# An attention stage written as 32 steps with a fixed order on each engine

## The chip, the cores and the metric

The kernel runs on one core of a Trainium2 chip. The metric is the time of one execution in device microseconds, the median of several runs. TensorE (PE in the profile) multiplies and transposes, and writes only to PSUM, here eight banks of 128 x 512 float32; VectorE (DVE) and ScalarE (ACT) read PSUM and work beside it; GpSimd (POOL) works on SBUF alone. SyncE (SP) issues most DMAs, GpSimd some. Each engine runs its own list of instructions one after the other and waits at semaphores for the others. The names DVE, ACT, POOL, PE, PEld (TensorE's weight loads) and SPq are those of the profile.

## What is computed

One layer of an encoder over 1024 rows of 1024 float32: half a SwiGLU, a mixer, half a SwiGLU, a norm. The change lies in the second part of the mixer.

```python
x = x + 0.5 * swiglu_half_step(x, ffn1_norm, ffn1_w_in, ffn1_w_out)
x = x + hybrid_mixer(x, ...)          # concatenate([attn, rec]) @ w_out
x = x + 0.5 * swiglu_half_step(x, ffn2_norm, ffn2_w_in, ffn2_w_out)
x = rms_norm(x, final_norm)

s = einsum('bqkgd,bskd->bkgqs', q_blk, k)      # 4 query heads, 2 key heads of 128
o = einsum('bkgqs,bskd->bqkgd', softmax(s), v)
attn = rms_norm(o, attn_out_gain)              # over the 512 columns of all heads
rec = rms_norm(recurrence) * silu(g)           # four heads of 128 columns
```

## The kernel before, in words

Every float32 product is made of three matmuls on rounded halves (high x high, high x low, low x high), so nearly every evacuation of PSUM is a pair: ScalarE copies or scales the high half (`hi`), VectorE subtracts it from the source for the low half (`lo`).

The program is written in order and planned by the framework's scheduler at build time: it lists instructions by priority (the order of the text, with stretches under `high_priority` ahead) and fills engines as its own time estimate has them free. What the engines execute is that order. `behind(x)` (line 96) adds an edge: an instruction is issued after `x` on the same engine. A tile pool hands out its buffers by tag; a tile waits until the buffer's former tile is done with.

The stage around the change:

- `mixer_in` (line 1043) ends the input projections. Its last one, `rg_av`, makes four parts (`rgv_ps`, line 831) in PSUM tag `pp` (four banks) and empties each with a Silu of the recurrence's gate (`gate`, line 1081) and a split of v into `v_attn` (line 1120). The gate goes through one of two buffers of `st` and is stored by SyncE (line 1086).
- `attention` (line 1132) opens its pools over that memory: SBUF starts with two buffers `rg` on the two of `st`, then `x1` (one), `rT`, three `p`, `qT`, `qr`; in PSUM two banks of tag `b` and two of tag `o` on the old `pp`, and two double banks `pp` for the scores.
- 32 pairs `seq[i] = (tp, n, tt)`: four blocks `tp` of 256 query rows, four heads `n`, two halves `tt` of 128 rows. For each: six score matmuls into a `pp` tile, the maximum (VectorE, line 1187), the exponential (ScalarE, 1190), the reciprocal and the scaling of p by GpSimd (left half) and ScalarE (right half); two groups of four transposes of p through tag `b` (`transposed`, 1197, with copy and subtraction into pT); after two `tt` the product with v (`values`, 1208: 24 matmuls of 256 columns), whose sum of squares over the heads makes the norm (`attn_scale`, 1284). The scores of pair i + 2 stand ahead of the transposes of pair i.
- The output projection of the recurrence (`rec_out`, 1265) goes with pairs 0 to 7: load the rows of the four recurrence heads and of the gate into `rg`, multiply on GpSimd, transpose (`rT`, tag `o`), project with `w_out`'s lower half (`project`, 1233: two halves of twelve matmuls, tag `o`), add to the row block x1 and store as x2.
- The output projection of attention (`attn_out`, 1292) of block `tp` goes with the pairs of the next block: load x2, project with the upper half (`woa`, loaded and split at pairs 4, 6, 9 and 10), scale and add on VectorE, store x3 from GpSimd's queue; `to_ffn` (1308) norms the row block for the second FFN and stores xn2. The last two row blocks follow the loop.
- The queries of the next block are transposed as a whole in a `pp` tile (`q_tile`, 1158).
- Then the second FFN opens its own pools over all of this, loads xn2 and weights, and transposes the rows (`pt_ffn_B`).

## Time and profile before

| | |
|---|---|
| median of three runs | 1928.17 us (1928.05 to 1928.54) |
| the profiled execution | 1929.75 us; its span, first to last instruction, 1927.6 |
| granted clock of TensorE, mean | 0.999 |
| TensorE, weight loads, VectorE, ScalarE, GpSimd busy | 99%, 83%, 65%, 42%, 37% of the span |
| the attention stage | from about 1052 to 1276.6 us of the span |

How it is read: times count from the first instruction. A row of a timeline gives start, length, engine, line, operation, written and read tile, shape and count; in brackets stands how long the engine was idle before it and who ended that. A row of the waits gives the total, the number and the longest of one kind. A row of the chain is a piece of the path that ended last, in order of time. [...]

### The profile page before, as it was taken

How to read it: one execution, taken by the hardware profiler on the slowest of the kernel's cores; microseconds unless marked ns; L12 is line 12 of the kernel's file. 1: busy time of each engine (PE TensorE's matmuls, PEld its weight loads, DVE VectorE, ACT ScalarE, POOL GpSimd, SP SyncE). 2: the span in 40 equal slices, each digit the busy share in tenths (PEclk: the TensorE clock that was granted, in tenths of full speed). 3: DMA queues.
4: the chain of work that ended last, by engine and by line, in shares of the span. 5: the costliest groups of instructions: out<-in, count | busy, mean ns of one | idle time of the engine just before them, and what ended most of it. 6: DMA issues, size and time to landing. Idle time of an engine off the chain costs nothing.

```text
span 1927.6 us, 26292 instructions
## 1 busy us (share of the span) xinstructions
PE 1905.8 (99%) x10025; PEld 1597.7 (83%) x10025; DVE 1250.9 (65%) x1578; ACT 802.1 (42%) x1280; POOL 714.1 (37%) x561
## 2 busy tenths in 40 slices
PE   9999999999999999999999999999999999999998
...
DMA packets 212940, 254.78 MB, mean 132 GB/s; under 512 B 13495, under 2 KB 140748, under 8 KB 212814
## 3 DMA queue, kind: packets, MB, share of 16 engines
...
q8 instruction: 79, 1.29, 0.3%
...
## 4 chain that ended last, share of the span: by engine, by line
PE 90%; DVE 4%; DMA 3%; issue 1%; ACT 1%; POOL 0%; SPq 0%; DVEq 0%; POOLq 0%; ACTq 0%
PE pa_ffn L298 17%; PE pd_ffn L298 11%; PE pya_ffn L684 7%; PE rec_ps L166 6%; PE pc_ffn L298 6%; PE pb_ffn L298 6%; PE pp_ffn L280 5%; PE pye_ffn L684 3%; PE pyd_ffn L684 3%; PE pyc_ffn L684 3%; PE aq_ps L831 2%; PE ri_ps L831 2%; PE pa L1243 2%; PE rgv_ps L831 2%; PE pv L1215 2%; PE s L1183 2%
## 5 line engine op out<-in xcount | busy, mean ns | idle before, releaser
L94 DVE TENSOR_TENSOR hl_in_ffn_A<-raw_in_ffn,hl_in_ffn_A 128x512 fp32r<-128x512 f32 x120 | 177.4, 1478 | 94.0 <-ACT hl_in_ffn_A L93 93.9
L298 PE MATMUL pa_ffn<-ffn_T,hl_in_ffn_S 128*128 128x512 f32 x960 | 236.8, 389 | 0.0
L298 PE MATMUL pd_ffn<-ffn_B,hl_in_ffn_S 128*128 128x512 f32 x936 | 225.7, 389 | 0.0
L298 PEld LDWEIGHTS pa_ffn<-ffn_T,hl_in_ffn_S 128*128 128x128 f32 x960 | 180.2, 188 | 37.4
L298 PEld LDWEIGHTS pd_ffn<-ffn_B,hl_in_ffn_S 128*128 128x128 f32 x936 | 175.7, 188 | 36.4
L93 ACT CAST hl_in_ffn_S<-s_ffn 128x512 fp32r<-128x512 f32 x160 | 99.0, 622 | 212.2 <-PE pd_ffn L298 159.0
L94 DVE TENSOR_TENSOR hl_in_ffn_S<-s_ffn,hl_in_ffn_S 128x512 fp32r<-128x512 f32 x160 | 140.9, 885 | 70.7 <-ACT hl_in_ffn_S L93 70.5
L94 DVE TENSOR_TENSOR hl_out_ffn_A<-raw_out_ffn_A,hl_out_ffn_A 128x1024 fp32r<-128x1024 f32 (+1 forms) x66 | 101.6, 1551 | 48.1 <-ACT hl_out_ffn_A L93 47.3
L93 ACT CAST hl_in_ffn_A<-raw_in_ffn 128x512 fp32r<-128x512 f32 x120 | 74.9, 625 | 137.1 <-PE pc_ffn L298 70.8
L94 DVE TENSOR_TENSOR hl_out_ffn_S<-raw_out_ffn_S,hl_out_ffn_S 128x512 fp32r<-128x512 f32 (+1 forms) x88 | 101.6, 1162 | 40.7 <-ACT hl_out_ffn_S L93 40.7
L166 PE MATMUL rec_ps<-hm,hl_rec_w 128*128 128x512 f32 x528 | 123.1, 392 | 0.8 <-DVE hm L145 0.4
L254 POOL TENSOR_TENSOR s_ffn<-s_ffn,raw_in_ffn 128x512 f32<-128x512 f32 x40 | 63.5, 1587 | 159.5 <-issue 104.6
L684 PE MATMUL pya_ffn<-hl_out_ffn_S 128*128 128x512 f32 x528 | 120.9, 390 | 0.1
L298 PE MATMUL pa_ffn<-ffn_B,hl_in_ffn_A 128*128 128x512 f32 x480 | 116.9, 389 | 0.0
L684 PEld LDWEIGHTS pya_ffn<-hl_out_ffn_S 128*128 128x128 f32 x528 | 99.0, 188 | 21.4 <-DVE hl_out_ffn_S L94 1.0
L166 PEld LDWEIGHTS rec_ps<-hm,hl_rec_w 128*128 128x128 f32 x528 | 98.4, 188 | 21.7 <-DVE hm L145 0.8
L298 PE MATMUL pc_ffn<-ffn_T,hl_in_ffn_A 128*128 128x512 f32 x480 | 115.9, 389 | 0.0
L298 PE MATMUL pb_ffn<-ffn_B,hl_in_ffn_A 128*128 128x512 f32 x480 | 115.3, 389 | 0.0
L93 ACT CAST hl_out_ffn_S<-raw_out_ffn_S 128x512 fp32r<-128x512 f32 (+1 forms) x88 | 73.4, 837 | 95.7 <-PE pya_ffn L684 38.6
L298 PEld LDWEIGHTS pc_ffn<-ffn_T,hl_in_ffn_A 128*128 128x128 f32 x480 | 90.1, 188 | 18.7
L298 PEld LDWEIGHTS pb_ffn<-ffn_B,hl_in_ffn_A 128*128 128x128 f32 x480 | 90.1, 188 | 18.7
L298 PEld LDWEIGHTS pa_ffn<-ffn_B,hl_in_ffn_A 128*128 128x128 f32 x480 | 90.0, 188 | 18.7
...
## 6 DMA issues: line engine op xcount, KB each, us to landing
...
raw_out_ffn_S<-d_comb SPq DMA_DIRECT2D x88, 256.0 KB, 2.7
d_comb<-g_ffn POOLq DMA_DIRECT2D x80, 256.0 KB, 2.3
raw_out_ffn_A<-d_act SPq DMA_DIRECT2D x66, 256.0 KB, 5.1
ffn_kept<-in_ffn_w_out SPq DMA_DIRECT2D x65, 256.0 KB, 5.4
d_act<-g_ffn SPq DMA_DIRECT2D x60, 256.0 KB, 2.3
raw_out_ffn_A<-in_ffn_w_out SPq DMA_DIRECT2D x52, 256.0 KB, 5.4
...
```

The lines of the kernel that those rows point to most:

```text
L93: nc.scalar.copy(hl[:, 0, :], src)
L94: (lo_engine or nc.vector).tensor_sub(hl[:, 1, :], src, hl[:, 0, :].bitcast(F32))
L166: nc.tensor.matmul(out, hl[:, a, ks], h[half][b][:, k, cols], start=(k == 0 and i == 0), stop=(k == NK - 1 and i == 2),)
L254: nc.gpsimd.tensor_sub(s2, s1, a11)
L280: nc.tensor.matmul(halves(ps[j]), A[2 * j + k // 4][:, a, ks], B[k // 4][:, :, b, k % 4, lo:hi], start=(k == 0 and i == 0), stop=(k == NK ...
L298: nc.tensor.matmul(ps, A[:, a, ks], op(key)[:, b, k, :], start=(first and k == 0 and i == 0), stop=(k == 3 and i == 2), skip_group_check=True,
L684: nc.tensor.matmul(ps, hl[:, a, j * P : (j + 1) * P], hl[:, b, hi], start=(first and i == 0 and n == 0), stop=(i == last and n == 2), skip ...
L831: nc.tensor.matmul(ps[:, tt, :], h[half][a][:, k, ts], hl[j][:, b, ws], start=(k == 0 and i == 0), stop=(k == NK - 1 and i == 2),)
L1183: nc.tensor.matmul(ps[:, ks], qT[:, a, qs], kT[:, b, kv, ks], start=(i == 0), stop=(i == 2))
L1215: nc.tensor.matmul(ps, vt[:, j, a, vs], pT[j][:, b, i4, :], start=(st == 0 and i == 0), stop=(st == NT - 1 and i == 2),)
L1243: nc.tensor.matmul(py, lhs(a, n), units[n][:, b, ds], start=(n == 0 and i == 0), stop=(n == 3 and i == 2),)
```

## The change

The 32 pairs become 32 steps, and each compute instruction of the loop is issued through `run`, which puts it behind the last one of its engine: the order of the text is the order on TensorE, VectorE, ScalarE and GpSimd. The prologue is issued through `free`, without that edge. DMAs are still placed by the scheduler. Each step gives the order: scores of step i + 2 (first half), first transposes, scores (second half), the product with v of the pair before (even steps, one step later than before), output halves, the transposes for the recurrence's next block and for the next block's queries, second transposes. Tables at the top say in which step what goes: the recurrence's blocks, the loads and the splits of `woa`, and each half of attention's output projection.

Besides: the queries are transposed in two halves through tag `b`, in the steps with i % 8 of 2 and 4; `values` uses tag `o` always; `x1` has two buffers; `woa` is loaded without the gate on a load, two or three steps ahead of its split; residual rows (x2) are asked for a step ahead of their use, those of the last two blocks in step 30 and behind the loop; the store of the gate's last two parts of the second column group goes by GpSimd's queue; the last two row blocks take three heads first and the fourth once the last product with v is there.

```diff
+REC_STEPS = (0, 1, 3, 4, 5, 7, 9, 11)
+WOA_LOADS = (2, 5, 8, 10)
+WOA_LATE = {4: 0, 7: 1, 11: 2, 12: 3}
+ATTN_HALVES = (13, 15, 16, 17, 19, 21, 23, 25, 27, 27, 29, 29)
...
-            nc.sync.dma_start(
+            (nc.gpsimd if (c, part // 2) == (1, 1) else nc.sync).dma_start(
...
+        last = {}
+        def run(engine, fn, *args, **kw):
+            with self.behind(last.get(engine)):
+                last[engine] = fn(*args, **kw)
+            return last[engine]
+        def free(engine, fn, *args, **kw):
+            return fn(*args, **kw)
+        def lows(do, lo, src, hi):
+            do("dve", nc.vector.tensor_sub, lo, src, hi.bitcast(F32))
+        def request(r0, j, name):
+            raw = self.wpool.tile([P, 1024], F32, name=f"raw_{name}{j}", tag="raw")
+            nc.sync.dma_start(raw, w_out[r0 + j * P : r0 + (j + 1) * P, :])
+            return raw
+        def cast(raw, j, pool, tag):
+            hl = pool.tile([P, 2, 1024], F32R, name=f"hl_woa{j}", tag=tag)
+            run("act", nc.scalar.copy, hl[:, 0, :], raw)
+            lows(run, hl[:, 1, :], raw, hl[:, 0, :])
+            return hl
...
-            pt = self.ps(f"qTp{tp}")
...
+        def q_turn(do, tp, raw, half, tag):
+            pt = self.ps(f"qTp{tp}_{half}", tag)[:, :512]
+            for m in range(2):
                 for tt in range(2):
+                    i = tt * 512 + (2 * half + m) * P
+                    at = slice(m * 256 + tt * P, m * 256 + (tt + 1) * P)
+                    do("pe", nc.tensor.transpose, pt[:, at], raw[:, i : i + P], self.ident)
+            hi, lo = (qT[tp][:, j, half * 512 : (half + 1) * 512] for j in range(2))
+            def evacuate():
+                do("act", nc.scalar.copy, hi, pt)
+                lows(do, lo, pt, hi)
+            return evacuate
...
+        def scores(do, a, j):
+            if j == 0:
+                a.ps = self.ps(f"s{a.nm}")
+            ks = slice(j * 512, (j + 1) * 512)
+            for i, (x, y) in enumerate(((0, 0), (0, 1), (1, 0))):
+                do("pe", nc.tensor.matmul, a.ps[:, ks], qT[a.tp][:, x, a.qs], kT[:, y, a.kv, ks],
+                   start=(i == 0), stop=(i == 2))
+        def small(a, what):
+            return self.stat.tile([P, 1], F32, name=f"{what}{a.nm}", tag=what)
+        def exponential(do, a):
+            neg_max, a.den = small(a, "nmax"), small(a, "den")
+            do("dve", nc.vector.tensor_reduce, neg_max, a.ps, AX.X, ALU.max, negate=True)
+            a.p = s4(f"p{a.nm}", "p")
+            do("act", nc.scalar.activation, a.p, a.ps, AF.Exp, bias=neg_max, accum_out=a.den)
+        def inverse(do, a):
+            a.rd = small(a, "rd")
+            do("dve", nc.vector.reciprocal, a.rd, a.den)
+            do("pool", nc.gpsimd.tensor_scalar_mul, a.p[:, 0:512], a.p[:, 0:512], a.rd)
+        def scaled(do, a):
+            do("act", nc.scalar.mul, a.p[:, 512:], a.p[:, 512:], a.rd)
+        def turned(a, j):
+            pt = self.ps(f"ptp{a.nm}_{j}", "b")
             for t in range(4):
                 i = (j * 4 + t) * P
+                run("pe", nc.tensor.transpose, pt[:, t * P : (t + 1) * P], a.p[:, i : i + P], self.ident)
             src = pt.rearrange("p (s t) -> p s t", t=P)
+            hi, lo = (a.pT[:, j, i, :, a.tt * P : (a.tt + 1) * P] for i in range(2))
+            def evacuate():
+                run("act", nc.scalar.copy, hi, src)
+                lows(run, lo, src, hi)
+            return evacuate
+        def values(a):
...
+            def evacuate():
+                run("act", nc.scalar.mul, hi, ps, g)
+                run("dve", nc.vector.scalar_tensor_tensor, out=lo, in0=ps, scalar=g, in1=hi.bitcast(F32),
+                    op0=ALU.mult, op1=ALU.subtract)
+                if a.n == 0:
+                    run("act", nc.scalar.activation, sq, ps, AF.Square)
+                    return
+                s1 = pools["sq"].tile([P, 256], F32, name=f"sq{a.nm}", tag="sq")
+                run("act", nc.scalar.activation, s1, ps, AF.Square)
+                engine = ("dve", nc.vector) if a.tp == 3 else ("pool", nc.gpsimd)
+                run(engine[0], engine[1].tensor_add, sq, sq, s1)
+            return evacuate
+        def half_out(py, lhs, units, ds, heads=range(4)):
+            for n in heads:
+                for i, (x, y) in enumerate(((0, 0), (0, 1), (1, 0))):
+                    run("pe", nc.tensor.matmul, py, lhs(x, n), units[n][:, y, ds],
+                        start=(n == 0 and i == 0), stop=(n == 3 and i == 2))
...
+        def rec_turn(t):
+            rg = rows[t][0]
+            run("pool", nc.gpsimd.tensor_mul, rg[:, 0:512], rg[:, 0:512], rg[:, 512:])
             pt = self.ps(f"rT{t}", "o")
             for n in range(NREC):
                 ns = slice(n * P, (n + 1) * P)
+                run("pe", nc.tensor.transpose, pt[:, ns], rg[:, ns], self.ident)
+            rT = recT[t] = pools["rT"].tile([P, 2, 512], F32R, name=f"recT{t}", tag="rT")
+            def evacuate():
+                run("act", nc.scalar.mul, rT[:, 0, :], pt, self.rec_gain)
+                run("dve", nc.vector.scalar_tensor_tensor, out=rT[:, 1, :], in0=pt, scalar=self.rec_gain,
+                    in1=rT[:, 0, :].bitcast(F32), op0=ALU.mult, op1=ALU.subtract)
+            return evacuate
+        def rec_half(t, dd):
+            py = self.ps(f"py{t}_{dd}", "o")
+            half_out(py, lambda x, n: recT[t][:, x, n * P : (n + 1) * P], rec_units, cols(dd))
+            x1 = rows[t][1][:, cols(dd)]
+            def evacuate():
+                run("dve", nc.vector.tensor_add, x1, py, x1)
+                if dd:
+                    nc.sync.dma_start(d["x2"][t], rows[t][1])
+            return evacuate
+        def out_scale(tp, do=run, tag="o"):
             pss = self.ps(f"oss{tp}", tag)
             for tt in range(2):
+                do("pe", nc.tensor.matmul, pss[:, tt : tt + 1], ssq[tp][:, tt * P : (tt + 1) * P], self.ones,
+                   start=True, stop=True)
+            work = self.stat.tile([P, 2, 2], F32, name=f"rs_ao{tp}", tag="rs2")
+            scale[tp] = work[:, 1, :]
+            def evacuate():
+                do("dve", nc.vector.tensor_scalar, work[:, 0, :], pss[:, 0:2], 1.0 / (NQ * HD), EPS,
+                   ALU.mult, ALU.add)
+                do("pool", nc.gpsimd.tensor_tensor, out=work[:, 1, :], in0=work[:, 0, :],
+                   in1=self.neg_half[:, :2], op=ALU.pow)
+            return evacuate
+        def row(t):
+            rows[NT + t] = x = s4(f"x2_{t}", "xs")
             nc.sync.dma_start(x, d["x2"][t])
...
+        def attn_half(t, dd):
+            py = self.ps(f"pa{t}_{dd}", "o")
+            half_out(py, lhs_attn(t), units, cols(dd))
+            def evacuate():
+                attn_add(t, dd, py)
+                if dd:
+                    nc.gpsimd.dma_start(d["x3"][t], rows[NT + t])
+            return evacuate
+        def to_ffn(t):
+            x = rows[NT + t]
             xn = pools["xn"].tile([P, D], F32, name=f"xn_n2_{t}", tag="xn")
+            ss = self.stat.tile([P, 1], F32, name=f"ss_n2_{t}", tag="ss1")
+            run("act", nc.scalar.activation, xn, x, AF.Square, accum_out=ss)
+            work = self.stat.tile([P, 2, 1], F32, name=f"rs_n2_{t}", tag="rs1")
+            run("dve", nc.vector.tensor_scalar, work[:, 0, :], ss, 1.0 / D, EPS, ALU.mult, ALU.add)
+            run("pool", nc.gpsimd.tensor_tensor, out=work[:, 1, :], in0=work[:, 0, :],
+                in1=self.neg_half[:, :1], op=ALU.pow)
+            def finish():
+                run("dve", nc.vector.scalar_tensor_tensor, out=xn, in0=x, scalar=work[:, 1, :], in1=gain2,
+                    op0=ALU.mult, op1=ALU.mult)
+                nc.gpsimd.dma_start(d["xn2"][t], xn)
+            return finish
...
+        waiting, finishing, raw_q, raw_w = None, [], None, {}
         for i, (tp, n, tt) in enumerate(seq):
+            a, u = steps[i], i % 8
+            ahead = step(i + 2) if i + 2 < len(seq) else None
             if tt == 0:
+                pT = self.hpool.tile([P, 2, 2, 4, 256], F32R, name=f"pT{a.nm}", tag="h")
+            a.pT = pT
+            if u == 0 and tp < 3:
+                raw_q = q_load(tp + 1)
+            if i in WOA_LOADS:
+                j = WOA_LOADS.index(i)
+                raw_w[j] = request(0, j, "woa")
+            if i == 0:
+                rec_turn(0)()
+            if tp and u == 2:
+                out_scale(tp - 1)()
+            if ahead:
+                scores(run, ahead, 0)
+            turned(a, 0)()
+            if ahead:
+                scores(run, ahead, 1)
+            if i and i + 1 < len(seq):
+                scaled(run, steps[i + 1])
+            if ahead:
+                exponential(run, ahead)
+            after = []
+            if tt == 0 and waiting:
+                after.append(values(waiting))
+                waiting = None
+            outs = []
+            if i in REC_STEPS:
+                t = REC_STEPS.index(i)
+                if t + 1 < NT:
+                    rows[t + 1] = rec_loads(t + 1)
+                outs = [rec_half(t, dd) for dd in range(2)]
+            elif i in ATTN_HALVES:
+                outs = [attn_half(*divmod(m, 2)) for m, at in enumerate(ATTN_HALVES) if at == i]
+            later = []
+            if i + 1 in REC_STEPS:
+                later.append(rec_turn(REC_STEPS.index(i + 1)))
+            if tp < 3 and u in (2, 4):
+                later.append(q_turn(run, tp + 1, raw_q, u // 2 - 1, "b"))
+            tb = turned(a, 1)
+            for f in outs:
+                f()
+            if ahead:
+                inverse(run, ahead)
+            for f in (*after, *((tb, *later) if tt else (*later, tb)), *finishing):
+                f()
+            finishing = []
+            if i + 1 in ATTN_HALVES[::2]:
+                row(ATTN_HALVES[::2].index(i + 1))
+            if i - 1 in ATTN_HALVES[1::2]:
+                finishing.append(to_ffn(ATTN_HALVES[1::2].index(i - 1)))
+            if i == len(seq) - 2:
+                row(2 * tp)
+            if i in WOA_LATE:
+                j = WOA_LATE[i]
+                units.append(cast(raw_w.pop(j), j, *(gate if j == 3 else whl)))
+            if tt:
+                waiting = a
+        t0 = 2 * (len(seq) // 8 - 1)
+        wide = {}
+        row(t0 + 1)
+        for t in (t0, t0 + 1):
+            wide[t] = self.ps(f"pa{t}")
+            for dd in range(2):
+                half_out(wide[t][:, cols(dd)], lhs_attn(t), units, cols(dd), range(3))
+            if t == t0:
+                values(waiting)()
+        for dd in range(2):
+            half_out(wide[t0][:, cols(dd)], lhs_attn(t0), units, cols(dd), (3,))
+        out_scale(t0 // 2, run, "b")()
+        for dd in range(2):
+            attn_add(t0, dd, wide[t0][:, cols(dd)])
+        nc.gpsimd.dma_start(d["x3"][t0], rows[NT + t0])
+        for dd in range(2):
+            half_out(wide[t0 + 1][:, cols(dd)], lhs_attn(t0 + 1), units, cols(dd), (3,))
+        for dd in range(2):
+            attn_add(t0 + 1, dd, wide[t0 + 1][:, cols(dd)])
+        nc.gpsimd.dma_start(d["x3"][t0 + 1], rows[NT + t0 + 1])
...
-                c3, tc, "m2", rg=2, x1=1, rT=1, p=3, qT=2, qr=1
+                c3, tc, "m2", rg=2, x1=2, rT=1, p=3, qT=2, qr=1
```

## The prediction, made before the changed kernel ran

> **What bounds the kernel now.** The page comes first: its span and its line of TensorE.

> ```profile
> span 1927.6 us, 26292 instructions
> PE 1905.8 (99%) x10025; PEld 1597.7 (83%) x10025; DVE 1250.9 (65%) x1578; ACT 802.1 (42%) x1280; POOL 714.1 (37%) x561
> ```

> The profiled execution took 1929.75 us, 1.58 above the median of the three runs (1928.17); a difference worked out on the trace is added to that median at the end. TensorE is the bound from end to end: an edit can only win what TensorE idles, and costs whatever makes it idle anew. About 0.2% (3.9 us) is what a measurement of this kernel can tell from no change. The change leaves the count of matmuls and transposes alone and orders the attention stage anew, so next comes the stage by itself: busy time by windows, then who TensorE waited for in it.

> ```profile
> 1052.00:1276.60 224.60, 218.01 (x1293) 188.59 (x1292) 137.39 (x212) 123.18 (x221) 77.98 (x70) 1.00 0.41 136
> ```

> ```profile
> PE ptp L1202 <- DVE pT L1206: 3.2, 5, 1.0
> PE s L1183 <- ACT p L1190: 1.0, 2, 0.7
> PE rT L1271 <- issue: 0.9, 1, 0.9
> PE pv L1215 <- DVE pT L1206: 0.7, 2, 0.3
> PE pa L1243 <- ACT oT L1221: 0.6, 1, 0.6
> ```

> The columns behind the length (224.60) are the busy times of TensorE, its weight loads, VectorE, ScalarE and GpSimd. TensorE idles 224.60 - 218.01 = 6.6 us here, and half of it is one wait: the transposes of the probabilities (ptp) wait for VectorE to empty one of the two banks of tag `b`. The true loss is somewhat more. A matmul's record overhangs the start of the next one, so each wait shows short by the overhang. The chain in order of time gives the real pitch:

> ```profile
> 1119.09 2.78 DMA d_x<-x
> 1121.93 5.46 DMA x<-d_x
> ...
> 1161.70 2.88 PE pv L1215 x24
> 1164.58 2.75 PE pa L1243 x12
> ...
> 1173.51 0.87 PE ptp L1202 x8
> ```

> So TensorE spends 2.88 on a `values`, 2.75 on half an output projection (twelve matmuls; so 0.69 on three score matmuls of the same 512 columns), 0.44 on four transposes. Eight transposes are recorded as 1.04 (below) and pitch at 0.87: 0.17 of overhang. Eleven waits in the five rows times 0.17 are 1.9; 6.6 + 1.9 = **8.5 us** is what a perfect order could win, 0.44% of the run. Its ends are 6.6 and about 10 (waits too short for the view).

> **Part 1, what goes.** The two DMA rows above show the store of x2 and then the load of the next x1 standing in the chain, because `x1` has one buffer; the change gives it two and asks for the `woa` rows up to three steps before their split. That, and most of the five rows, is curable by an order. I credit the whole 8.5 and then charge the waits of the new order one by one.

> **Part 2, the entry.** TensorE's new queue begins with the transposes rT(0) into a bank of tag `o`, and everything else of the loop stands behind them. Tag `o` lies on the banks of the last rgv part (pool order: b, o over the old `pp`), which is emptied late:

> ```profile
> 1054.29 2.89 PE L1183 MATMUL s<-kT,qT 128*128 128x512 f32 x12
> 1055.11 0.36 SPq L1086 DMA_DIRECT2D d_g<-rg  x1
> 1055.59 0.69 DVE L94 TENSOR_TENSOR v_attn<-rgv_ps,v_attn 128x512 fp32r<-128x512 f32 x1 [0.91 <-ACT v_attn L93]
> 1058.00 1.80 SPq L1258 DMA_DIRECT2D rg<-d_rec  x4
> 1059.84 0.43 SPq L1260 DMA_DIRECT2D rg<-d_g  x1
> 1064.78 1.29 POOL L1267 TENSOR_TENSOR rg<-rg 128x512 f32<-128x512 f32 x1 [1.32 <-DMA rg<-d_g]
> ```

> Before, twelve score matmuls filled the time from 1054.29. Now they are queued behind rT(0), which waits until 1055.59 + 0.69 = 1056.28, plus 0.13 of release (below): **2.1 us** of idle, with the prologue's other work already done inside rgv.

> The gate stores are costed next. SyncE no longer waits for the last two Silus, so the rows of rg(0) and the second half of k are asked for some us sooner; they are covered by the rgv matmuls, and that is worth nothing to TensorE. But rg(1) lies on the buffer of the last gate part: its load (1058.00) follows that store (1055.11) by 2.9. GpSimd's stores of the same size land like SyncE's:

> ```profile
> d_comb<-g_ffn POOLq DMA_DIRECT2D x80, 256.0 KB, 2.3
> d_act<-g_ffn SPq DMA_DIRECT2D x60, 256.0 KB, 2.3
> ```

> So rg(1) comes when it came. Its last piece takes 3.7 as a median and took up to 1064.78 - 1059.84 = 4.9 here:

> ```profile
> rg<-d_g SPq DMA_DIRECT2D x8, 256.0 KB, 3.7
> ```

> GpSimd multiplies it from 1063.5 to 1064.8 on, 1.29 later rT(1) can start: 1064.8 to 1066.1. TensorE is there at 1056.4 + 0.44 + 2 x 0.69 + 0.44 + 2 x 2.75 = 1064.2, and turned(0,1) is queued behind. Cost 0.7 to 2.0, I take **1.4**. [...]

> **Part 3, the queries in halves.** This is the largest term. The transposes of the next queries moved from `pp` to tag `b`: six times (steps 2, 4, 10, 12, 18, 20) three tiles pass through two banks between `values` and the next step's first transposes. Durations:

> ```profile
> 1240.59 1.13 ACT L1190 ACTIVATE p<-s,nmax 128x1024 f32<-128x1024 f32 x1
> 1241.50 1.22 DVE L1187 TENSOR_REDUCE nmax<-s 128x1 f32<-128x1024 f32 x1
> 1247.45 0.47 ACT L1221 ACTIVATE oT<-pv,cols 128x256 fp32r<-128x256 f32 x1 [1.27 <-PE pv L1215]
> 1249.86 0.40 ACT L1230 ACTIVATE sq<-pv 128x256 f32<-128x256 f32 x1
> 1251.91 1.04 PE L1202 MATMUL ptp<-ident,p 128*128 128x128 f32 x8
> 1252.54 1.07 ACT L1205 CAST pT<-ptp 128x512 fp32r<-128x512 f32 x2 [1.60 <-PE ptp L1202]
> 1253.16 1.29 DVE L1206 TENSOR_TENSOR pT<-ptp,pT 128x512 fp32r<-128x512 f32 x2 [1.67 <-ACT pT L1205]
> 1258.57 1.28 DVE L125 SCALAR_TENSOR_TENSOR xn_n<-x,rs_n,g_ffn_norm 128x1024 f32<-128x1024 f32 x1 [0.70 <-POOL rs_n L86]
> 1260.17 1.28 DVE L1206 TENSOR_TENSOR pT<-ptp,pT 128x512 fp32r<-128x512 f32 x2
> 1260.99 1.16 PE L1202 MATMUL ptp<-ident,p 128*128 128x128 f32 x8 [0.18 <-DVE pT L1206]
> ```

> The fourth transpose of 1251.91 is issued by 1252.35 and ScalarE starts at 1252.54: 0.19. VectorE's subtraction starts 0.62 after the copy and takes 0.69, two of them 1.29 (pitch 0.60). TensorE starts 1260.99 after a subtraction that ended at 1260.86: 0.13. Clock an even step from 0. TensorE: scores 0.69, first transposes 1.13, scores 1.82, `values` 4.70, queries 5.14, second transposes 5.58, next scores 6.27; then the next transposes want the bank of the queries. ScalarE, in its fixed order: copy 1.32; VectorE's subtraction 1.94, maximum 2.54 to 3.76; exponential 3.8 to 4.9; oT 4.93; square 5.3; only then the queries' copy at 5.66, subtraction 6.28 to 6.97, release 7.1. TensorE idles 7.1 - 6.27 = 0.83. That is the floor, 6 x 0.83 = 5.0. In steps 2 and 10 the recurrence's rT (the same 512 columns, one more on each engine) stands in front: about 1.2 each. In step 4 two halves give the engines time, but rT stays in front: 1.0. In step 12 the split of woa2 left over from step 11 (1024 columns, about 1.1 and 1.2 as in the rows of that width above) delays the exponential: 1.9. In 18 and 20 the xn row of 1.28 stands on VectorE ahead of the step's first subtraction: 1.5 each. Sum 8.3 with these lags, 5.0 without; I take **6.5**, the middle, since each lag may be eaten by the stall before it. All other steps hold: two tiles through two banks, a bank wanted five us after it was written.

> [...]

> **Part 4, the last steps.** In step 31 nothing is left to put between: second transposes of step 30, first of 31, second of 31. With `values` ending at V, ScalarE does oT, square and the copy from V + 0.92 on, subtraction V + 1.54 to V + 2.2, release V + 2.35; TensorE is there at V + 0.87. Cost **1.4** (0.8 if ScalarE is ahead). After it nothing waits: the three first heads of row 6, the last `values`, the three first heads of row 7 cover each other's evacuations by 4.1 us of matmuls (eighteen at the pitch above).

> **Part 5, the start of the second FFN.** Row 7's load stands on SyncE until the xn row of 5 is done, and FFN 2's first loads stand behind it, as before:

> ```profile
> 1248.41 11.83 SPq L1296 DMA_DIRECT2D x<-d_x  x2
> 1260.34 0.85 SPq L1545 DMA_DIRECT2D xn<-d_xn  x2
> ...
> 1264.34 3.81 SPq L1545 DMA_DIRECT2D xn<-d_xn  x1
> ...
> 1276.18 1.91 PE L442 MATMUL pt_ffn_B<-ident,xn 128*128 128x128 f32 x16
> ```

> Before, they start at 1260.34, 15.8 ahead of the first transposes of FFN 2. Now that xn row is finished in step 31. From the end of row 5's last half: step 30's copy ends at 5.2, the square of row 5 at 6.4, two more copies 7.6, their subtraction 8.4, xn 9.7. TensorE from there to the end of the stage: five groups of transposes and a `values` 5.1, the 1.4, then 36 + 12 matmuls, a `values` and the sums 14.3, together 20.8; so the loads start some 11 ahead. Against that the wait of 3.81 goes: `x1` has one more buffer, so xn row 2 lands on `rT`'s old place and no longer on a `p` still in use. The first four loads come 4.8 later, the rest about 1. What of that TensorE feels no row shows; between nothing and half the shift, 0 to 2.5, I take **0.6**, nearer to nothing since the weights wait longest for their use.

> Sum: 2.1 + 1.4 + 6.5 + 1.4 + 0.6 = 12.0 of new waits against 8.5 of old ones: **+3.5 us**, 1933.2 for a profiled execution, **1931.7** against the median. The bounds together: 2.1 + 0.7 + 5.0 + 0.8 + 0 - 10 = -1.4 to 2.1 + 2.0 + 8.3 + 1.4 + 2.5 - 6.6 = +9.7.

> **Rivals.** *The order pays.* The queries' bank comes free in time, because ScalarE reaches their copy sooner than I clock it, and rT(1) too; only the entry and 0.7 stay: 2.1 + 0.7 - 8.5 = -5.7, 1922.5. For it: ScalarE is 55% busy in the stage (123.18 of 224.60), and the waits that go are real. Against it: even an idle ScalarE needs 0.19 + 0.62 + 0.69 + 0.13 = 1.63 where TensorE has 1.13 of other work. Chance 0.2.

> *FFN 2's loads decide.* The place is SyncE's queue behind row 7. If the first weights land more than a microsecond behind the end of attention, TensorE waits for each microsecond beyond; the price is the shift of 4.8 on top of the forecast: +8.3, 1936.5. For it: the queue stood 11.83 us in the same place. Against it: the 3.81 that goes. Chance 0.2.

> **How the numbers follow.** The forecast (0.6) is +3.5 with bounds of -1.4 and +9.7; as +3.9 is the limit, I give 0.34 of it to no change and 0.26 to slower. With the rivals: faster 0.20, same 0.34, slower 0.20 + 0.26 = 0.46. The likeliest time is 1931.7. The range goes from 1922.5, which leaves out half of the first rival, to 1937.5, which leaves out under 0.1 above. No change and slower hold most of the chance; the forecast's own range is 1926.8 to 1937.9.

> **What would show it.** Right: the timeline after shows TensorE idle for some 2 us ahead of the first rT, one wait of 0.8 to 1.9 at the first transposes of steps 3, 5, 11, 13, 19 and 21, each ended by a subtraction of qT, and one of 1.4 in step 31; the store and load of x1 are out of the chain; the stage's idle time is 10 us or more. Wrong: the row of ptp waiting for qT is short or absent (then the first rival), or a DMA ends a wait over a microsecond anywhere after step 1 (then the order meets the queues, and the sum is too low).

## The result, and the profile after

The changed kernel is **slower by 1.1%**: 1949.05 us median (1946.35 to 1952.09) against 1928.21 (1928.05 to 1928.54), ratio 1.0108, 95% interval 1.0091 to 1.0126. The forecast was 1931.7 with a range of 1922.5 to 1937.5. The profiled execution took 1952.09, the longest of its four, so the trace below shows some 3 us more than the median. (The four took 1952.09, 1949.41, 1948.68 and 1946.35, at a mean granted clock of 0.993, 0.995, 0.996 and 0.997.) Of all executions below one alone falls out, 6245.39 us in the version with some attention halves moved, without a trace; the ratio there leaves it out.

The page of the changed kernel, its span and busy line:

```profile
span 1950.3 us, 26280 instructions
PE 1912.5 (98%) x10025; PEld 1601.9 (82%) x10025; DVE 1247.8 (64%) x1582; ACT 803.1 (41%) x1284; POOL 721.7 (37%) x563
```

The work of TensorE is the same, the span 22.7 us longer. The attention stage by windows, columns as before (length; busy time of TensorE, its weight loads, VectorE, ScalarE, GpSimd; granted clock):

```profile
1052.00:1298.00 246.00, 225.42 (x1299) 192.97 (x1297) 138.01 (x215) 125.71 (x227) 81.18 (x71) 0.97 0.35 120
```

The stage idles 246.00 - 225.42 = 20.6 us instead of 6.6, and TensorE is busy for 225.4 instead of 218.0 on the same work, at a granted clock of 0.97 instead of 1.00. Both are losses. Whom it waited for (all instructions issued through `run` bear its line, L1145; one goes by tiles):

```profile
PE ptp L1145 <- DVE qT L1145: 6.9, 4, 3.2
PE ptp L1145 <- POOL ssq L1145: 4.2, 2, 2.2
PE rT L1145 <- POOL rg L1145: 3.2, 1, 3.2
PE pt_ffn_B L446 <- DVE x L1145: 2.9, 2, 2.3
PE ptp L1145 <- DVE pT L1145: 1.3, 1, 1.3
PE rT L1145 <- issue: 0.8, 1, 0.8
PE py L1145 <- DVE x L1145: 0.8, 1, 0.8
```

The first two rows are the queries' bank, six times, as forecast, in the steps forecast (in two of them a GpSimd addition ended within 0.1 us of the subtraction of qT and got the name; with the queries in another bank, below, these two waits go as well, though the addition stays). The row of 3.2, five times, by which the kernel before waited for pT is down to one wait, that of step 31, and the store and load of x1 are out of the chain.

To add the losses up I take, for each instruction on TensorE, the distance from the start of the one before it, less the median of that distance for its kind (a wait measured so is called "by starts" below); the sum from the start of the stage to the second FFN's first transposes is 10.9 us before and 28.7 after, in the next 60 us 1.5 and 5.9. That is 22.2 of the 22.7. After, it is mainly: the entry 3.35, the queries' six waits 12.1 (1.67, 0.81, 1.74, 2.40, 3.35, 2.13), three waits for a bank of tag `o` or for recT 2.6, step 31 1.9, the start of the second FFN 3.6 in three waits; and matmuls that run at half pace behind some of these waits, 7.4 in the stage and about 2 in the second FFN. The half pace is in the windows. Three of four and six microseconds, right behind the waits of 1.74, 2.40 and 3.35 (the third column from the end is the granted clock):

```profile
1150.10:1154.10 4.00, 4.00 (x20) 3.39 (x21) 2.35 (x3) 2.06 (x3) 0.00 (x0) 1.00 0.00 0
1166.00:1170.00 4.00, 4.00 (x14) 3.24 (x14) 3.25 (x4) 2.12 (x4) 0.00 (x0) 0.57 0.00 0
1205.00:1211.00 6.00, 6.00 (x18) 4.86 (x19) 2.37 (x4) 2.95 (x6) 0.58 (x1) 0.54 0.01 3
```

### The profile page after: what moved, and what is told of

It is laid out like the page before. It is cut to its first block, busy times and chain, and to the rows that moved or that the text cites. A ratio compares the mean times of both kernels' runs of the same rounds, so it can differ in the third digit from the quotient of the medians.

```text
span 1950.3 us, 26280 instructions
## 1 busy us (share of the span) xinstructions
PE 1912.5 (98%) x10025; PEld 1601.9 (82%) x10025; DVE 1247.8 (64%) x1582; ACT 803.1 (41%) x1284; POOL 721.7 (37%) x563
## 3 DMA queue, kind: packets, MB, share of 16 engines
q8 instruction: 79, 1.29, 0.3%
## 4 chain that ended last, share of the span: by engine, by line
PE 91%; DVE 4%; ACT 2%; DMA 1%; issue 1%; POOL 1%; SPq 0%; DVEq 0%; POOLq 0%; ACTq 0%
PE pa_ffn L302 17%; PE pd_ffn L302 11%; PE pya_ffn L688 9%; PE rec_ps L170 6%; PE pb_ffn L302 6%; PE pc_ffn L302 6%; PE pp_ffn L284 5%; PE pye_ffn L688 3%; PE pyc_ffn L688 3%; PE pyb_ffn L688 3%; PE pyd_ffn L688 3%; PE aq_ps L835 2%; PE ri_ps L835 2%; PE py L1145 2%; PE rgv_ps L835 2%; PE pa L1145 2%
## 5 line engine op out<-in xcount | busy, mean ns | idle before, releaser
L688 PEld LDWEIGHTS pya_ffn<-hl_out_ffn_S 128*128 128x128 f32 x528 | 99.1, 188 | 20.8 <-DVE hl_out_ffn_S L98 0.3
## 6 DMA issues: line engine op xcount, KB each, us to landing
raw_out_ffn_S<-d_comb SPq DMA_DIRECT2D x88, 256.0 KB, 2.7
d_comb<-g_ffn POOLq DMA_DIRECT2D x80, 256.0 KB, 2.3
raw_out_ffn_A<-d_act SPq DMA_DIRECT2D x66, 256.0 KB, 4.9
ffn_kept<-in_ffn_w_out SPq DMA_DIRECT2D x65, 256.0 KB, 5.3
d_act<-g_ffn SPq DMA_DIRECT2D x60, 256.0 KB, 2.3
raw_out_ffn_A<-in_ffn_w_out SPq DMA_DIRECT2D x52, 256.0 KB, 5.4
```

What stands on the lines that cost most here:

```text
L688: nc.tensor.matmul(ps, hl[:, a, j * P : (j + 1) * P], hl[:, b, hi], start=(first and i == 0 and n == 0), stop=(i == last and n == 2), skip ...
```

## The experiments

The theory: (a) the queries' transposes in tag `b` cost the six waits, made longer by a chain on ScalarE and VectorE that the forecast did not count; (b) TensorE's clock falls behind a wait of more than about 2 us (an estimate from the windows above: 1.00 behind the 1.74, 0.57 behind the 2.40, 0.54 behind the 3.35) and doubles the price; (c) the entry, (d) row 7's load at the start of the second FFN, (e) step 31. Rivals: the order written out by hand costs as such, and a mended wait comes back elsewhere; the half pace belongs to places, not to waits; DMA queues decide. All ratios are to the kernel before.

### The queries' bank: another bank, another order on ScalarE, more cover

```diff
-                later.append(q_turn(run, tp + 1, raw_q, u // 2 - 1, "b"))
+                later.append(q_turn(run, tp + 1, raw_q, u // 2 - 1, "pp"))
```

> One edit to the changed kernel: the next queries' halves are transposed into a tile of the wide tag (pp) instead of the two-bank tag b. Theory (three tiles through two banks cost 12.1 us of waits for the queries' subtraction in steps 3, 5, 11, 13, 19 and 21, and the clock drops that follow the longest of them cost about 5 more): the row of ptp waiting for qT disappears, 1949.0 - 12.1 - 5 = about 1932. Rival 1 (the waits cost only their own length; the doubled pitch after them comes from something else): 1937. Rival 2 (the fixed order of all engines or the DMA queues cost the time, and a wait mended here comes back at the next one): 1945 or more.

Measured 1939.07, ratio 1.0051 (1.0036 to 1.0066): 10.0 below the changed kernel (the profiled executions differ by 12.9). The waits for qT are gone, and so is every lowered clock from step 1 to the end of the stage (mean clock of the profiled execution 0.996, against 0.993). New is one row, scores that wait for the exponential because the queries hold a slot of `pp`:

```profile
PE s L1145 <- ACT p L1145: 3.1, 3, 1.5
```

It came out 7 above the theory's 1932: 3.6 are this new wait by starts, and about 3 come from the sum itself, which took the half pace of the profiled execution off a median that is 3 us lower. By the time alone the first rival (1937) is nearer; the trace decides against it, since no half pace is left where the waits are gone. The second rival's 1945 is excluded.

```diff
+            if tp < 3 and u in (2, 4):
+                later.pop()()            # copy and subtraction of qT ahead of oT and its square
```

> The changed kernel with one change of order on ScalarE and VectorE alone: in the six steps with queries, their copy and subtraction come ahead of the evacuation of the values (oT and its square). The bank stays in tag b. Theory (the waits were half as long again as forecast because the square on ScalarE waits for VectorE's subtraction of the same bank, and the queries' copy stands behind it): each of the six waits falls by 1.0 to 1.5 us, the sum from 12.1 to about 4, none is over 2 us and the clock drops behind them go: 1949.0 - 8 - 4.5 = about 1936. Rival (three tiles through two banks cost this whatever the order of the other engines): the sum stays over 10, 1946 or more.

Measured 1943.43, ratio 1.0069 (1.0053 to 1.0086). By starts the six waits are 0.43, 0.43, 0.43, 1.10, 2.00 and 1.97, together 6.4 instead of 12.1, none with a lowered clock behind it (mean clock 0.997). The chain on ScalarE was half of them; the sum of 4 was too hopeful, since in steps 18 and 20 the exponential ahead of the copy is late as well. The time fell by 5.6, of the 13 expected, and lies between the theory's 1936 and the rival's 1946; the sum of 6.4 excludes the rival's "over 10". The stage itself is 9.9 shorter: from the start of the input projections' last matmul to the second FFN's first transposes it takes 230.36 us in this trace and 240.27 in the changed kernel's, but it began 2.3 later. (That start lies between 1053.67 and 1056.36 in the twenty traces, though the kernels hardly differ ahead of it.)

```diff
+            if ahead and tp < 3 and u in (3, 5):
+                scores(run, ahead, 1)
             turned(a, 0)()
-            if ahead:
+            if ahead and not (tp < 3 and u in (3, 5)):
                 scores(run, ahead, 1)
```

> The changed kernel with one change of TensorE's order alone: in steps 3, 5, 11, 13, 19 and 21 the second half of the scores goes ahead of the first transposes, so 0.69 us more work lies in front of the bank that is waited for. Theory: each wait falls by 0.69, the sum from 12.1 to 8.0, the longest from 3.35 to 2.7; the clock drop behind the waits of 2.1 and 2.4 goes and that behind the longest may stay: 1949.0 - 4.1 - 1 to 3 = 1942 to 1944. If the doubled pitch had nothing to do with the waits: 1945. Rival (the wait is set by something that runs with TensorE, so cover gives nothing): 1949.

Measured 1944.55, ratio 1.0080 (1.0065 to 1.0095). The six waits are 1.00, 0.12, 1.04, 1.71, 2.66 and 1.41, together 7.9; a lowered clock stands behind the 2.66 alone (0.57 from 1199 to 1203). Cover of 0.69 in each of the six took 4.2 off the waits, so it comes off one for one; the time alone does not tell the theory (1942 to 1944) from a half pace that has nothing to do with the waits (1945).

### The entry, and the gate's store

Row 0 of the recurrence one step later, on top of the queries in `pp`:

```diff
-REC_STEPS = (0, 1, 3, 4, 5, 7, 9, 11)
+REC_STEPS = (1, 2, 3, 4, 5, 7, 9, 11)
...
-                rec_turn(0)()
+                rows[1] = rec_loads(1)
```

> The queries in the wide tag as in the run beside it, and the recurrence's first transposes no longer stand ahead of step 0: row 0 of the recurrence is projected in step 1, its transposes go between step 0's scores and its second transposes. Theory: the 3.2 us at the entry shrink to under 1 and the doubled pitch of the ten matmuls behind it (about 2 us) goes too: 3 to 5 us below the run beside it, about 1928. Rival (the wait at the entry only moves to step 1, because GpSimd's multiplication stays late): equal to the run beside it within 1.5 us.

Measured 1936.59, ratio 1.0038 (1.0025 to 1.0051), 2.5 below the run without it: the wait is 1.35 instead of 3.20, and no clock falls there (mean clock 0.998, against 0.996 without the edit). It is less than the 3 to 5 expected because a new pair of waits came with it, 0.78 and 0.83 at the recurrence's next block, where tag `o` is short of a bank: here a mended wait did come back in part. Why the entry was longer than the 2.1 of the forecast is in the changed kernel's timeline,

```profile
1055.18 0.73 POOL L1090 DMA_DIRECT2D d_g<-rg  x1 [10.08 <-ACT rg L1088]
1055.39 0.69 DVE L98 TENSOR_TENSOR v_attn<-rgv_ps,v_attn 128x512 fp32r<-128x512 f32 x1 [0.92 <-ACT v_attn L97]
1056.12 1.25 POOL L1145 TENSOR_TENSOR rg<-rg 128x512 f32<-128x512 f32 x1 [0.21 <-DMA rg<-d_g]
1057.43 1.11 PE L1145 MATMUL rT<-ident,rg 128*128 128x128 f32 x4 [3.18 <-POOL rg L1145]
```

and in the chain in order of time:

```profile
1052.55 3.31 DMA rg<-d_g
1056.12 1.26 POOL rg L1145
```

The bank is free at 1055.39 + 0.69 = 1056.08, as forecast; but the rows have to be multiplied first. Their last piece landed at 1052.55 + 3.31 = 1055.86, GpSimd was held by its store until 1055.91, and the multiplication takes 1.25 from 1056.12 on. So GpSimd's store is not what is late there, as the next expectation still has it: without the multiplication the bank would have let the transposes start more than a microsecond sooner. Giving the store back to SyncE:

```diff
-            (nc.gpsimd if (c, part // 2) == (1, 1) else nc.sync).dma_start(
+            nc.sync.dma_start(
```

> The changed kernel with the last gate parts stored by SyncE's queue again, as before the change. Theory (the wait of 3.2 us at the entry is GpSimd's multiplication of row 0, which stood behind the 0.73 us of its own store): with SyncE storing, the loads of row 0 of the recurrence and of the second half of k stand behind the last two Silus instead, row 0's last piece lands about 2 us after that, and the entry becomes longer: 4 to 6 us, so 1950 to 1952. Rival (GpSimd's queue is all that is late there): the multiplication starts 0.7 earlier, the entry falls to 2.4 and 1948.

Measured 1953.51, ratio 1.0126 (1.0110 to 1.0143), 4.5 above the changed kernel and more than the theory's 1950 to 1952; the entry's wait is 7.31. SyncE waits for the last Silu, and row 0's own loads stand behind it:

```profile
1056.65 0.36 SPq L1090 DMA_DIRECT2D d_g<-rg  x1
1057.10 1.85 SPq L1286 DMA_DIRECT2D rg<-d_rec  x4
1061.98 1.26 POOL L1145 TENSOR_TENSOR rg<-rg 128x512 f32<-128x512 f32 x1 [17.33 <-DMA rg<-d_rec]
1063.30 1.12 PE L1145 MATMUL rT<-ident,rg 128*128 128x128 f32 x4 [7.31 <-POOL rg L1145]
```

The store by GpSimd, to which the forecast gave nothing, is worth 4.5 us in this order, because rT(0) stands first in TensorE's queue.

### The clock: pauses put in on purpose

Eight one-column matmuls, in a version with few waits (the second of "all together", below), that read a late result:

```diff
+PAUSE = {6: "den", 8: "p", 10: "rd", 14: "p", 22: "den", 24: "p", 26: "den", 28: "nmax"}
...
+                run("pe", nc.tensor.matmul, self.ps(f"pause{i}", "o")[:, 0:1], self.ident, src,
+                    start=True, stop=True)
```

> The run beside it with eight pauses put into TensorE's queue: in steps 6, 22 and 26 a one-column matmul that reads the sum of the exponentials of the step ahead (about 2.6 us after its scores), in step 28 one that reads the maximum (about 1.5), in step 10 one that reads the reciprocal (about 2.9), in steps 8, 14 and 24 one that reads what GpSimd has scaled (about 4). The output is unchanged; the time of the pauses is added work. Theory (TensorE's granted clock falls when it has idled for more than about 2 us): the matmuls behind the pauses of 2.6 to 4 us run at twice their pitch (0.43 instead of 0.23) for 2 to 6 us, those behind the pause of 1.5 do not, the granted clock of the run is 0.99 or less, and the run is longer by the pauses (about 22) and some 10 us more. Rival (the doubled pitch belongs to the place, not to the wait): the pitch behind all of them stays 0.23, and the run is longer by the pauses alone.

Measured 1989.77, one execution, 51.6 above the same version without them. The pauses became 2.69 to 6.89 us long, together 36.0; behind each of the eight TensorE ran at half pace, 13.8 in all, while the version without them has no lowered clock in the stage (mean clock 0.985 with the pauses, 0.996 without). So the half pace belongs to the waits and not to the places. How short a wait may be, this run does not show: the pause meant as the short one, of about 1.5, became 2.69. The first pause by the timeline, and the windows of 4 us behind the pauses of 3.29 and 2.69:

```profile
1107.83 0.94 PE L1146 MATMUL s<-kT,qT 128*128 128x512 f32 x3
1111.90 0.38 PE L1146 MATMUL pause<-den,ident 128*128 128x1 f32 x2 [3.13 <-ACT p L1146]
1112.15 4.61 PE L1146 MATMUL pv<-pT,v_attn 128*128 128x256 f32 x24
```

```profile
1112.00:1116.00 4.00, 4.00 (x22) 4.00 (x23) 0.00 (x0) 0.00 (x0) 0.00 (x0) 0.60 0.40 131
1293.00:1297.00 4.00, 4.00 (x23) 4.00 (x23) 0.00 (x0) 1.04 (x2) 0.00 (x0) 0.59 0.55 223
```

A `values` that pitches at 2.88 took 4.61. That it is the clock, and that one wait can have it and another not, shows in one wait of the same length in the same place of two kernels. The changed kernel, and the one with row 7 in wo (below):

```profile
1204.88 1.09 PE L1145 MATMUL ptp<-ident,p 128*128 128x128 f32 x4 [3.19 <-DVE qT L1145]
1205.62 1.63 PE L1145 MATMUL s<-kT,qT 128*128 128x512 f32 x3
1207.05 4.55 PE L1145 MATMUL pa<-hl_woa,oT 128*128 128x512 f32 x12
```

```profile
1204.54 0.63 PE L1145 MATMUL ptp<-ident,p 128*128 128x128 f32 x4 [3.19 <-DVE qT L1145]
1204.92 0.94 PE L1145 MATMUL s<-kT,qT 128*128 128x512 f32 x3
1205.69 2.92 PE L1145 MATMUL pa<-hl_woa,oT 128*128 128x512 f32 x12
```

What differs is how the wait lies to a grid. In the changed kernel's trace the lowered clock starts at 1056.97, 1166.19, 1203.74, 1220.81 and 1299.31, which is 32, 11, 5 and 23 lengths of 3.41 us apart; in the other kernel's execution the grid lies 0.51 us elsewhere (1203.23 against 1203.74). Cut by it, the changed kernel's wait left TensorE busy for 1.37 of the 3.41 us ahead of 1203.74, the other kernel's for 1.54 (first the changed kernel, two lengths each; behind the length comes the busy time, then the clock):

```profile
1200.33:1203.74 3.41, 1.37 (x10) 1.00 0.86 282
1203.74:1207.15 3.41, 2.27 (x8) 0.50 0.00 1
```

```profile
1199.81:1203.23 3.42, 1.54 (x11) 1.00 0.86 278
1203.23:1206.64 3.41, 2.10 (x12) 1.00 0.07 26
```

The last section counts this.

### The order itself, and the second buffer of x1

```diff
-            with self.behind(last.get(engine)):
-                last[engine] = fn(*args, **kw)
-            return last[engine]
+            return fn(*args, **kw)
```

> The changed kernel with the order on the engines left to the scheduler: the helper that chains each engine's instructions no longer does so; tiles, tags and steps as changed. Theory (the loss is three tiles in two banks and single late operations, which a scheduler can only partly go round): between 1935 and 1945. Rival (the order written out by hand is what costs): at most 1930, as before.

Measured 1937.00, ratio 1.0042 (1.0027 to 1.0057). This is inside the theory's range, and the rival (at most 1930) is excluded. With the order left to the scheduler the stage loses 11.2, like before; the second FFN loses 9.2. The order as written costs 12 us; that an order by hand must, the last runs below deny.

The kernel before with `x1=2` and nothing else:

> The kernel before with one part of the change alone: tag x1 has two buffers instead of one. The forecast credited the change with all of the 8.5 us that TensorE idled in the attention stage; of these the store of x2 and the load of the next x1 behind it stood in the chain at 1119 to 1128 and gave waits of about 2 us. Theory: 1 to 2.5 us faster, 1926 to 1927.5. Rival (the scheduler's order was made for one buffer, and the wait is only moved on): within 1 us of the kernel before.

Measured 1933.35, ratio 1.0022 (1.0012 to 1.0032): not faster but **4.6 us slower**, outside both expectations. The stage loses 11.0 (10.9 before), the second FFN's first 60 us lose 4.6 (1.5 before), which is 3.1 of the 4.6; the rest lies ahead of the stage, whose start wanders by more than that (above). The second buffer moves all that lies behind it in SBUF, and with it what the second FFN's tiles may have to wait for. To test this, the same with the second buffer behind the other left-hand pools:

```diff
-            x1 = s4(f"x1_{t}", "x1")
+            x1 = s4(f"x1_{t}", "x1b" if t % 2 else "x1")
...
-                c3, tc, "m2", rg=2, x1=1, rT=1, p=3, qT=2, qr=1
+                c3, tc, "m2", rg=2, x1=1, rT=1, p=3, qT=2, qr=1, x1b=1
```

> The kernel before with a second buffer for x1, this time placed last among the left-hand pools, so that the second FFN's tiles lie where they lay. Theory (the 4.6 us that the second buffer cost in the kernel before came from the shifted places: the load of xn row 3, asked for ahead of row 6 in the kernel before, moved behind it): 1926.5 to 1929, the kernel before or a little faster. Rival (the second buffer itself changes the scheduler's order for the worse): 1932 or more, as with the shifted places.

Measured 1928.89, ratio 1.0003 (0.9994 to 1.0012): the kernel before. SyncE's rows show the difference, first of the kernel with `x1=2`, then with x1b:

```profile
1221.06 40.69 SPq L1296 DMA_DIRECT2D x<-d_x  x3
1261.86 2.19 SPq L1545 DMA_DIRECT2D xn<-d_xn  x2
```

```profile
1224.78 0.32 SPq L1545 DMA_DIRECT2D xn<-d_xn  x1
1248.11 11.83 SPq L1296 DMA_DIRECT2D x<-d_x  x2
```

With the places kept, one xn row is loaded at 1224.78, ahead of rows 6 and 7; with them shifted all four stand behind. That the places are the cause is shown, since x1 has its second buffer in both; the way from the late load to the 3.1 us is not: TensorE's waits in that run stand at 1304 to 1312 and are ended by VectorE. And mending x1's wait in the stage gained nothing here: the loss in the stage is about 11 in all three.

### The start of the second FFN: row 7

The changed kernel's rows (VectorE, SyncE, TensorE):

```profile
1288.32 3.60 SPq L1339 DMA_DIRECT2D x<-d_x  x1
...
1297.21 1.41 DVE L1145 SCALAR_TENSOR_TENSOR x<-pa,rs_ao,x 128x512 f32<-128x512 f32 x2 [1.98 <-DMA x<-d_x]
...
1298.67 0.66 PE L446 MATMUL pt_ffn_B<-ident,xn 128*128 128x128 f32 x4 [2.30 <-DVE x L1145]
```

Row 7 is asked for at 1288, its sums wait for it, and the next transposes wait for the sums' banks. Asked for in step 26, it needs another buffer. Three places were tried:

```diff
+            if i == len(seq) - 6:
+                row(2 * tp + 1, "x1")        # next: a buffer of wo; last: "xn"
...
-        row(t0 + 1)
```

> The changed kernel with one edit: row 7 of the residual is asked for in step 26, into a buffer of tag x1 that has been free since step 11, instead of in the last step into a buffer of xs that row 5 holds. Theory (the second FFN's first transposes wait 0.73 + 2.30 for the PSUM banks of row 7's sums, and these for row 7's load, which stands on SyncE behind row 5's normalization): both waits fall to under 0.8 together, 1949.0 - 2.5 = about 1946.5. Rival (the second FFN starts late because of its own weights, which are asked for late): the idle time stays, 1949; or, with the queue of SyncE free, the weights come earlier and that too is gained: 1945.

Measured 1964.23, ratio 1.0182 (1.0167 to 1.0197): 15 us worse. TensorE waits 12.6 us for the second FFN's first xn row.

> The changed kernel with one edit: row 7 asked for in step 26 as in the run that became slower, but into a buffer of wo instead of one of x1. Theory (row 7's late load costs the second FFN's start 2.5 us, and the 15 us lost in that run came from the x1 buffer, over which the second FFN's first xn tile lies): 1949.0 - 2.5 = about 1946.5, the waits of pt_ffn_B for x gone. Rival (asking early for row 7 is itself the harm): 1955 or more.

Measured 1957.39, ratio 1.0152 (1.0134 to 1.0171): the wait is now 10 us for ScalarE's copy of ffn_B. A first reading, that xn row 3 stood on SyncE behind row 6 of x3, was tried by chaining these loads:

> The run with row 7 in a buffer of wo, with one edit: the second FFN's loads of xn rows 0 to 3 are chained in that order on SyncE, ahead of its second weight tile and of the late rows. Theory (the 10.1 us of waiting for ScalarE's copy of ffn_B came because the load of xn row 3 stood on SyncE behind that of row 6 of x3, which waits for the end of attention): that wait falls to under 1 and the time from 1957.4 to about 1947, below the changed kernel by the 2.5 us of row 7's load. Rival (the buffer under xn row 3 comes free late, whatever the queue): 1955 or more.

Measured 1956.45, ratio 1.0141 (1.0128 to 1.0155), and still 8.0 of wait: that reading fell. The third place:

> The changed kernel with one edit: row 7 asked for in step 26 into a free buffer of tag xn. Theory: neither the 8 to 14 us wait of the other two places (x1, wo) nor the changed kernel's 2.3 us wait for row 7's load: 1949.0 - 2.5 = about 1946.5. Rival (asking early is the harm, wherever the row lies): 1955 or more, as in those.

Measured 1945.04, ratio 1.0083 (1.0069 to 1.0096): 4.0 below the changed kernel, the row of pt_ffn_B down to

```profile
PE pt_ffn_B L446 <- DVE x L1145: 0.8, 2, 0.6
```

By their times the two runs with wo fell where the rival put them (1955 or more); this run excludes it. So asking early is right, and worth about 4: the ranges of the two kernels' executions overlap (1943.01 to 1947.26, 1946.35 to 1952.09), and in the traces 3.3 us of it stand at the start of the second FFN, whose first 200 instructions on TensorE take 25.36 instead of 28.69. What cost 8 to 15 us was the buffer. The cause stands in the rows of a run with row 7 in wo (the chained one of the next part; ScalarE, GpSimd, and the DMA view's line for the store with its time from issue to landing):

```profile
1282.04 1.66 ACT L392 CAST hl_in_ffn_A<-raw_in_ffn 128x512 fp32r<-128x512 f32 x3 [14.68 <-issue]
```

```profile
1275.27 0.53 POOL L1498 DMA_DIRECT2D d_x<-x  x1 [0.74 <-DVE x L1145]
```

```profile
d_x<-x POOLq DMA_DIRECT2D x2, 512.0 KB, 6.7
```

A weight tile of the second FFN lies over that buffer: ScalarE's cast begins when the store of row 7 has landed (1275.27 + 6.7 = 1281.97), though its weights had been asked for at 1260.60, and the copies of ffn_B stand behind the cast. In all six runs with row 7 in wo it begins 0.06 or 0.07 us behind that landing (without the chain, for one, at 1299.43 behind 1299.37). The traces list a wait for that store's semaphore with the casts of this tile; in the run with xn no early cast has one.

### All together

All mends: the entry with step 0's second transposes ahead of rT(0), the queries in `pp` and `o`, the values emptied ahead of output halves, nine matmuls of row 6 inside step 31, row 7 early.

> All mends together on the fixed order: row 0 of the recurrence projected in step 1 with step 0's second transposes ahead of its own; the queries' halves in the wide tag in steps 2, 4 and 10 and in tag o in steps 12, 18 and 20; the values' evacuation ahead of that of the output halves; row 7 loaded in step 26 into a free buffer of x1; nine matmuls of row 6 between the two groups of transposes of step 31. Theory (the loss is the sum of these single waits): from 1936.6 of the run with the queries in the wide tag and the entry mended go the rest of the entry 0.4, the two pairs of waits for a bank of tag o in the steps 2 and 4 (3.9), the scores' waits for a slot of the wide tag (3.6), step 31 (1.9) and the start of the second FFN (3): 1936.6 - 12.8 = about 1924, faster than the kernel before. Rival (the fixed order on all engines has a price of its own, one mended wait comes back as another): 1930 or more.

Measured 1946.49, ratio 1.0089 (1.0074 to 1.0104). By its time this is the rival's (1930 or more), but not for its reason: the stage loses 6.9 (10.9 before), its clock is 1.00, and row 7's place in x1 takes 14.2 + 3.0 at the second FFN.

> The run with all mends, with two of its buffers elsewhere: row 7 of the residual goes into a buffer of wo (free since step 11) and the second buffer of x1 stands last among the left-hand pools, so that the tiles of the second FFN lie over the same ones as in the kernel before. Theory (the 14 us of waiting for xn at the start of the second FFN came because its first xn tile lies over the x1 buffer that row 7 held to the end; with the attention stage at 6.9 us of losses against 8.9 before): the 14.2 and the 3.0 behind it fall to about 4 together, 1946.5 - 14 = about 1932, and down to 1927 if all of the second FFN's start is as in the kernel before. Rival (the early load of row 7 itself holds up SyncE's queue and the weights): 1940 or more.

Measured 1938.15, ratio 1.0047 (1.0029 to 1.0065): row 7 in wo costs 8.1 there. The stage, cut by the same two instructions as above, takes 218.46 us, against 222.12 before and 240.27 in the changed kernel.

> The run with all mends and the old places of the buffers, with the second FFN's xn loads chained in the same way. Theory: the 8.1 us of waiting for ffn_B fall to under 1: 1938.2 - 8 = about 1930, the time of the kernel before within 2 us, since the attention stage loses 7 us here and 9 there, and the wait for row 6's and 7's sums (2 us) stays. Rival (the weights behind the late rows are late in their turn): 1934 or more.

Measured 1938.47, ratio 1.0047 (1.0034 to 1.0060): no change. Of the theory's 8 us nothing came, and the time is in the rival's range (1934 or more). The rows of ScalarE and GpSimd above are of this run. With some attention halves moved:

```diff
-ATTN_HALVES = (13, 15, 16, 17, 19, 21, 23, 25, 27, 27, 29, 29)
+ATTN_HALVES = (14, 15, 16, 17, 21, 22, 23, 25, 27, 27, 29, 29)
```

> The run beside it, with the halves of rows 0 and 2 one or two steps later: row 0's first in step 14 instead of 13, row 2's in 21 and 22 instead of 19 and 21. Theory: the waits of 0.8 for the split of woa3 and of 1.4 for a bank of tag o in step 19 go: 1 to 2 us below the run beside it, 1928. Rival (the work moved out of step 19 was the cover of another wait): no difference, or up to 2 us more.

Measured 1942.52, ratio 1.0069 (1.0055 to 1.0082): 4 us worse, the rival's direction and more than its 2. The trace has three new waits of transposes for pT, 3.9 together. The matmuls moved had been their cover.

> The run with all mends and the chained loads of the second FFN, with row 7 in a free buffer of tag xn (under which only the second FFN's late rows lie), the scale of the last output rows asked for 12 matmuls sooner, and row 1's normalization held back from step 19 to step 21. Theory (each 8 us wait was a cast of the second FFN's first weights held by row 7's store): 1938.5 - 8.3 = 1930, and 1 to 2.5 less by the two small edits: about 1928.5, the time of the kernel before. If the attention stage's 7 us of losses fall to 5.5 as meant, 1927. Rival (the early load of row 7 itself): 1936 or more.

Measured 1933.58, ratio 1.0024 (1.0015 to 1.0033): slower than the theory's 1928.5 and below the rival's 1936. The profiled execution took 1934.72 at a clock of 0.999. The second FFN's first 60 us lose 2.6. But row 7 sits in one of two buffers of xn, and row 5's square has to wait until row 4 has left the other; ScalarE stands, and TensorE with it:

```profile
1267.05 1.06 ACT L1145 ACTIVATE xn_n<-x 128x1024 f32<-128x1024 f32 x1 [6.34 <-DMA d_xn<-xn_n]
```

```profile
PE pv L1145 <- ACT pT L1145: 4.0, 1, 4.0
```

Without that wait it would be near the time of the kernel before (1933.6 - 4.0 = 1929.6, an estimate); none of the versions that ran beats it.

## Why the prediction was wrong, point by point

Two steps of the prediction carry most of the error: the walk along ScalarE in part 3 came to little more than half its real size, and the clock was not in the sum at all. Term by term, in us, against the profiled execution and by starts:

| term | forecast | measured |
|---|---|---|
| the entry | 2.1 | 3.35 |
| rT(1) | 1.4 | 0 |
| the queries' six waits | 6.5 | 12.1 |
| step 31 | 1.4 | 1.9 |
| the start of the second FFN | 0.6 | 3.6 |
| waits for a bank of tag `o` or for recT | none | 2.6 |
| half pace of TensorE | none | 9.4 |
| shorter waits, the remainder | none | 1.65 |
| all that the kernel before loses there | -8.5 | -12.4 |
| sum | +3.5 | +22.2 |

- **Part 1, the credit of 8.5.** The old waits went, and the second buffer of x1 did what was said in the stage; the loss they made was even larger than read, 10.9 in the stage. But new short waits that the sum does not have came with the order (2.6 and 1.65), and no version kept the whole credit: the best fixed order still loses 6.9. The buffer has a price of its own in the kernel before, +4.6 when it alone is added, +0.0 when the places behind it are kept. In the changed kernel that price is not seen: instructions 200 to 800 of the second FFN on TensorE, where it stood, take 130.53 us there as before, against 133.63. The forecast looked at places only for xn row 2.
- **Part 2, the entry: 2.1, measured 3.35.** The bank came free when it said. The failed step is "the prologue's other work already done": row 0's load had only just landed, and its multiplication, 1.25, was not in the sum. The gate store "worth nothing to TensorE" failed too: taking it back costs 4.5, because row 0's load then lands later. rT(1), 1.4, cost nothing: its rows landed sooner than taken, its multiplication began at 1062.82 instead of 1063.5 or later, and TensorE itself came later.
- **Part 3, the queries: 6.5, measured 12.1**, above even its upper bound of 8.3. Mechanism, steps and releaser right; the walk along ScalarE was mis-sized. It set the square 0.4 behind the start of oT on ScalarE; in step 18 that is 1.08 (1202.07 to 1203.15). In the trace:

```profile
1199.67 1.21 DVE L1145 TENSOR_REDUCE nmax<-s 128x1 f32<-128x1024 f32 x1
...
1200.97 1.11 ACT L1145 ACTIVATE p<-s,nmax 128x1024 f32<-128x1024 f32 x1 [3.05 <-DVE nmax L1145]
...
1202.07 0.47 ACT L1145 ACTIVATE oT<-pv,cols 128x256 fp32r<-128x256 f32 x1
...
1202.57 0.48 DVE L1145 SCALAR_TENSOR_TENSOR oT<-pv,cols,oT 128x256 fp32r<-128x256 f32 x1 [0.20 <-ACT oT L1145]
...
1203.15 0.38 ACT L1145 ACTIVATE ssq<-pv 128x256 f32<-128x256 f32 x1 [0.61 <-DVE oT L1145]
1203.43 0.58 ACT L1145 CAST qT<-qTp 128x512 fp32r<-128x512 f32 x1
1204.04 0.69 DVE L1145 TENSOR_TENSOR qT<-qTp,qT 128x512 fp32r<-128x512 f32 x1 [0.99 <-ACT qT L1145]
```

  ScalarE's square reads the bank that VectorE's subtraction reads, and waits for it: 0.61 idle, and a hand-over from ScalarE to VectorE and back ahead of the queries' copy. In this step the maximum is late as well, behind the xn row, and ScalarE idles 3.05 before the exponential: the lags add up, they do not eat each other as "the middle" assumed. Emptying the queries first halves the sum (6.4). In 15 of the changed kernel's 16 products with v ScalarE's square begins 0.03 or 0.09 us behind the end of that subtraction: the two engines read the bank in turn, and the 0.61 is that turn's price here.
- **Part 4, step 31: 1.4, measured 1.49** (and 0.45 at the group before it, which the sum does not have). Right.
- **Part 5, the second FFN: 0.6, measured 3.6, and worth about 4 when mended.** The place was named, in this part and in the second rival, but for the weights. It was row 7, which stands behind the xn row of 5 in the same queue: the forecast quoted that row, asked what comes later for the weights, and not for row 7 itself.
- **Left out: the clock.** Idle time was charged at its own length. About 9.4 of the 22 us are half pace behind waits (7.4 in the stage, about 2 in the second FFN); the median execution has some 3 us less in all. The first sign of wrong, a wait over a microsecond ended by a DMA, came with row 7. The kernel before, whose longest wait in the stage is 1.1, never pays it.
- **The rivals.** *The order pays* had no part in it. *FFN 2's loads decide* had the place, SyncE's queue behind row 7, but not the load, and not the size. That the order as such costs is excluded by the versions that lose less in the stage than the kernel before.
